# Inverse roots and key products moved from GpSimd to VectorE, and a written TensorE order of nineteen places rearranged, in a hybrid recurrent decoder step

## The chip, the cores and the metric

The kernel runs on one core of one Trainium2 chip. The metric is device time in microseconds for one launch. Three runs of the kernel before took 2502.68, 2503.41 and 2505.58 us. Engine names are those of the profile: PE is the matrix engine (TensorE), PEld its weight loads, DVE is VectorE, ACT is ScalarE, POOL is GpSimd, SP is SyncE, whose queue issues the transfers named here.

## The reference, cut to what matters

One layer of a decoder for 1024 prompt tokens and 8 x 4 sample tokens: a norm, a wide projection `w_in`, three token mixers side by side (gated DeltaNet, called A; RWKV-7, called B; a diagonal recurrence, called C), gates and output projection, then a feed-forward part. The change touches the two mixers that carry a matrix state:

```
def gated_delta_chunked(q, k, v, g, beta, S0):      # A: 4 heads of 128, after l2norm of q and k
    L = where(strict, einsum(kb, k) * decay, 0);  A = eye + L
    sol = triangular_solve(A, [v*beta, kb*exp(gc)], lower, unit_diagonal)
    ... scan over chunks: S = S*glast + kdec^T vnew ...
    o = o * rsqrt(mean(o*o) + EPS) * norm_g * silu(z)
def rwkv7_scan(r, w, k, v, kk, a, S0):               # B: 8 heads of 64, kk = l2norm(k * k_k)
    S = S*w + (S @ -kk) (kk*a)^T + v k^T;  o = S r
    o = (o - mean) * rsqrt(var + B_LN_EPS) * ln_w + ln_b ...
```

Three inverse square roots are in the chunked part: over the key norm of A, over the output norm of A, and over the group norm of B. The "beta products" of the change are the two scaled key matrices of B (`kk*a` and `k`, each times a growing exponential).

## The kernel before, in words

Matrix products in single precision are split in three (high times high, high times low, low times high), 128 x 352 columns each. The program has a start, the C mixer, then the chunked stretch of the A and B mixers, then the branch, output and feed-forward products. The change lies in the chunked stretch alone, from about 330 to 1480 us of the profile.

There the tokens are cut in segments, nine for each of two groups of heads (eight of 128 tokens and one of the 32 sample tokens), so 18 units of work. A unit consists of three Python generators: `rwkv_seg` (B, L1000), `gdn_seg` (A, L1282) and `tri` (the inverses of the triangular matrices of both, L906). Every `yield` ends a step. A fourth generator, the filler, hands out the big projection products that are not yet done, three 128 x 352 products at a time: first those that the second group of heads needs, then the gates.

A list `PLAN` (L1474) of 19 places says what the loop at L1478 emits in each place for the unit that is starting (`n`) and for the unit before it (`o`): `r`, `g` and `t` advance one generator by one step, and two filler steps (six products) follow in each place. The class `Ordered` (L249) pins the order of all matmuls: PE runs them exactly as written, so a matmul whose input is late holds all later ones. The other engines and the SP queue are ordered by a planner at build time; `o` steps and the inverse have high priority there. Each engine then runs its own queue in order.

The steps that matter, by their lines. B: r1 projections, decay and the products BK (L1078 to L1085); r2 the scores (BK against AR, L1091) and the masked matrix GM (L1095); r3 and r4 value terms; r5 to r10 the recurrence over two halves (state product, triangular product, state update; UV is written at L1185 and L1186, N at L1217 and L1218); the last part of r10 is the group norm with its root (L1227 to L1236); r11 transposes the normed output (L1242), gates it and stores it (L1245 to L1249). A: g1 transposes and the key root (L1318), g2 scores LA (L1339), g3 to g5 the state and the output root (L1423), g6 transposes and the gate (L1430). Inverse: `inv16_load` (L832) sends GM and LA through memory and reads 16 x 16 blocks (tile i16m), `inv16_solve` (L848) inverts the blocks on DVE (L858 to L886), stores them (L894) and reads them back (tile i16u, L897); t1 expands and transposes them (L923, L924) and makes the first product, t2 to t6 the rest. The step `unit` starts the loads of the next unit.

In the list before, numbered from 0, the scores r2 and `load` stand in place 7, r9 and g5 in place 6, r10 in place 8, `solve` in 11, g6 in 12, r11 in 14, t1 in 17 and t2 in 18; t3 to t6 stand in places 0 to 3 of the next round.

`rsqrt` (L641) starts from an integer estimate and makes three Newton steps, 13 instructions on two or four columns, all on POOL.

Of the kernel before, what the change touches and what calls it, by code (L numbers as in the profile page):

```python
# [10 lines left out]
I32 = mybir.dt.int32  # L11
AXX = mybir.AxisListType.X
AF = mybir.ActivationFunctionType
ALU = mybir.AluOpType
# [414 lines left out]
def build(tc, ap):  # L429
    nc = tc.nc  # L430
    with ExitStack() as ctx:
        k = K(tc, ctx, ap)
        V, A, P, T, S = k.V, k.A, k.P, k.T, k.S
# [195 lines left out]
        def big(n=NT):  # L629
            return k.tile(mp, [128, n], "a4", 6)  # L630
# [4 lines left out]
        def k1(shape=(128, SEG), tag="k1", bufs=6):  # L635
            return k.tile(mp, shape, tag, bufs)
# [4 lines left out]
        def rsqrt(x, shape, tag):  # L641

            yi = k.tile(mp, shape, "nwy" + tag, 2, I32)
            t = k.tile(mp, shape, "nwt" + tag, 1)
            P.tensor_scalar(out=yi, in0=x.bitcast(I32), scalar1=-0.5, scalar2=1597463007.0, op0=ALU.mult, op1=ALU.add)
            y = yi.bitcast(F32)
            for _ in range(3):
                P.tensor_tensor(out=t, in0=y, in1=y, op=ALU.mult)
                P.tensor_tensor(out=t, in0=t, in1=x, op=ALU.mult)
                P.tensor_scalar(out=t, in0=t, scalar1=-0.5, scalar2=1.5, op0=ALU.mult, op1=ALU.add)  # L650
                P.tensor_tensor(out=y, in0=t, in1=y, op=ALU.mult)
            return y

        def store_tail(dst, z, sv, hist):
# [27 lines left out]
        t = big()  # L682
# [10 lines left out]
        for b0, nb in ((0, 4), (4, 4), (8, 1)):  # L693
            n = 32 if b0 == 8 else 128
            ps = k.tile(k.pr, [128, 4, 128], "rr", 4)
            for j in range(nb):
# [12 lines left out]
                        in1=gla[:32, 8:9].to_broadcast([32, 8, 4]), op=ALU.mult)  # L709
# [290 lines left out]
        def rwkv_seg(R, seg, J):  # L1000

            s2, lora = R["s2"], R["lora"]
            if True:
# [9 lines left out]
                zr, zk, zv = k1(tag="zr", bufs=2), k1(tag="zk", bufs=2), k1(tag="zv", bufs=2)  # L1013
# [6 lines left out]
                kk, tt = k1(), k1()  # L1020
# [52 lines left out]
                og = k1(tag="og", bufs=2)  # L1073
# [3 lines left out]
                for i in range(2):  # L1077
                    A.activation(out=pr(av, i), in_=pr(av, i), func=AF.Identity, scale=k.p("bka", 2 * s2 + i), bias=k.d("oka", 2 * s2 + i))  # L1078
                V.tensor_tensor(out=ch(zk), in0=ch(zk), in1=ch(av), op=ALU.mult)
                for src, j, e in ((kk, 0, P), (zk, 1, V)):  # L1080
                    for h in range(2):
                        e.tensor_tensor(out=BK[H[h], 0:nb, j if h == 0 else 1 - j, 0:tl], in0=ch(src)[H[h]], in1=ch(ei)[H[h]], op=ALU.mult)
                V.tensor_tensor(out=ar(1), in0=ch(zr), in1=ch(eg), op=ALU.mult)
# [10 lines left out]
                for h in range(2):  # L1094
                    V.tensor_tensor(out=GM[:, h, 0:nb], in0=ph[h],  # L1095
                                    in1=k.c("gms" if samp else "gm").unsqueeze(1).to_broadcast([128, nb, 128]), op=ALU.mult)
# [53 lines left out]
                for b in range(nb // 2):  # L1150
# [43 lines left out]
                    if samp:  # L1194
                        yield
                        for i in range(2):
                            p2 = k.tile(pq, [128, 512], "sr", 1)
                            for q in range(2):
                                ux = k.tile(mp, [128, 2, 4, 64], "ux", 1)
                                for h in range(2):  # L1200
                                    P.tensor_tensor(out=ux[:, h], in0=UV[:, i, h].unsqueeze(1).to_broadcast([128, 4, 64]),
                                                    in1=k.c("uvm")[:, 4 * q:4 * q + 4].unsqueeze(2).to_broadcast([128, 4, 64]), op=ALU.mult)
# [30 lines left out]
                V.tensor_reduce(out=mv[:, 1], in_=sq, axis=AXX, op=ALU.add)  # L1233
                V.tensor_scalar(out=mv[:, 1], in0=mv[:, 1], scalar1=1.0 / 64, scalar2=GN_EPS, op0=ALU.mult, op1=ALU.add)
                rs = rsqrt(mv[:, 1], [128, nb], "r")
                V.tensor_tensor(out=O, in0=O, in1=rs.unsqueeze(2).to_broadcast([128, nb, 64]), op=ALU.mult)  # L1236
                yield
# [44 lines left out]
        def gdn_seg(R, seg, J):  # L1282
# [3 lines left out]
            if True:  # L1286
# [22 lines left out]
                for b in range(nb):  # L1309
# [6 lines left out]
                    A.copy(kv[:n, :, b], ps[:n].rearrange("p (j c) -> p j c", j=4)[:, 0:3:2])  # L1316
                V.tensor_scalar(out=ss, in0=ss, scalar1=0.25, scalar2=EPS, op0=ALU.mult, op1=ALU.add)
                rk = rsqrt(ss[:, 0], [n, nb], "g")  # L1318
                sl = k.tile(mp, [128, 3, 2], "gsl", 2)[:n]
                V.tensor_tensor(out=sl[:, 0], in0=rk, in1=rk, op=ALU.mult)  # L1320
# [100 lines left out]
                V.tensor_scalar(out=oss[:n, :nb], in0=oss[:n, :nb], scalar1=1.0 / 128, scalar2=None, op0=ALU.mult)  # L1421
                V.scalar_tensor_tensor(out=oss[:n, :nb], in0=ss[:, 1], scalar=128.0 * EPS, in1=oss[:n, :nb], op0=ALU.mult, op1=ALU.add)
                rs = rsqrt(oss[:n, :nb], [n, nb], "o")  # L1423
                for b in range(nb):
                    A.activation(out=oa[:n, b], in_=oa[:n, b], func=AF.Copy, scale=rs[:, b:b + 1])
# [38 lines left out]
        def unit(i):  # L1464
            J = {}
            u = dict(J=J, r=rwkv_seg(rb, SEGB[i % 9], J), g=gdn_seg(ra, SEGA[i % 9], J), t=tri(J))
            next(u["r"])
            next(u["g"])
            return u
# [1 line left out]

        PLAN = (("nr ot", 2), ("ng ot", 2), ("ot or", 2), ("ot or", 2), ("or og", 2), ("or og", 2), ("or og ng", 2), ("nr load", 2),  # L1474
                ("or unit", 2), ("nr", 2), ("nr", 2), ("solve", 2), ("og", 2), ("", 2), ("or", 2), ("", 2), ("", 2), ("nt", 2),
                ("nt", 2))
        new, old = unit(0), None
        for i in range(19):  # L1478
            after_ = None
            for what, f in PLAN:  # L1480
                for w_ in what.split():
# [132 lines left out]
        for g in range(NG):  # L1614
# [4 lines left out]
            for j in range(8):  # L1619
# [4 lines left out]
                                                  op=ALU.subtract)  # L1624
# [3 lines left out]
        for fb in range(8):  # L1628
# [29 lines left out]
            for g in range(NG):  # L1658
# [3 lines left out]
                for j0, nj in ((0, 3), (3, 3), (6, 2)):  # L1662
                    yo = k.tile(fa, [128, NT], "ahi", 5)[:, :nj * GW].rearrange("p (j t) -> p j t", j=nj)
                    for j in range(nj):
                        V.scalar_tensor_tensor(out=yo[:, j], in0=x2[j0 + j][:, gl(g)], scalar=k.p("gf", j0 + j), in1=rs,  # L1665
                                               op0=ALU.mult, op1=ALU.mult)
# [18 lines left out]
```

## Time and profile before

| of the profiled execution | value |
|---|---|
| device time of that execution | 2511.07 us |
| span, first to last instruction | 2509.3 us |
| median of the three timed runs | 2503.41 us |
| PE busy | 2183.4 us (87%) |
| DVE busy | 1178.8 us (47%), 2490 instructions |
| ACT busy | 816.8 us (33%) |
| POOL busy | 512.2 us (20%), 1213 instructions |

A busy share is the time in which an engine executed something. "PEclk" is the clock granted to PE as a share of full speed: 1.00 is the upper level (2.4 GHz), 0.50 the lower (1.2 GHz). In rows of the timeline the brackets at the end give how long the engine was idle before the row, and what ended the idle time; a row with x32 merges 32 instructions. The profiled execution is one of its kind, 0.3% above the median of the timed runs.

### The profile page before, as it was taken

How to read it: one execution, taken by the hardware profiler on the slowest of the kernel's cores; microseconds unless marked ns; L12 is line 12 of the kernel's file. 1: busy time of each engine (PE TensorE's matmuls, PEld its weight loads, DVE VectorE, ACT ScalarE, POOL GpSimd, SP SyncE). 2: the span in 40 equal slices, each digit the busy share in tenths (PEclk: the TensorE clock that was granted, in tenths of full speed). 3: DMA queues.
4: the chain of work that ended last, by engine and by line, in shares of the span. 5: the costliest groups of instructions: out<-in, count | busy, mean ns of one | idle time of the engine just before them, and what ended most of it. 6: DMA issues, size and time to landing. Idle time of an engine off the chain costs nothing. (4 is left out here: it accounts for less than half of the span.)

```text
span 2509.3 us, 42716 instructions
## 1 busy us (share of the span) xinstructions
PE 2183.4 (87%) x16939; PEld 2042.7 (81%) x16939; DVE 1178.8 (47%) x2490; ACT 816.8 (33%) x1915; POOL 512.2 (20%) x1213
## 2 busy tenths in 40 slices
PE   8999987776667677777777899999999999999997
PEld 7998986666556565666656799999999999999997
DVE  7453353555555544455445205747433433333336
ACT  5564342333333332243333222225221221221224
POOL 2013233333324223233343220013000000000003
PEclk9999996888887887888888899999999999999999
DMA  4114331222222222222221335433111111111114
GB/s 132 67 57 135 101 100 57 77 66 55 56 60 69 62 66 77 57 68 64 62 55 50 106 129 193 151 120 109 43 46 48 47 47 43 51 43 47 47 44 148
DMA packets 171713, 191.59 MB, mean 76 GB/s; under 512 B 60853, under 2 KB 114293, under 8 KB 171513
## 3 DMA queue, kind: packets, MB, share of 16 engines
q1 hardware_dynamic: 171512, 188.87, 24.6%
q8 instruction: 133, 2.18, 0.4%
q14 instruction: 68, 0.55, 0.1%
HBM read 140.68 MB, written 48.13 MB: 75 GB/s over the span
## 5 line engine op out<-in xcount | busy, mean ns | idle before, releaser
L259 PE MATMUL g<-hhi,whi 128*128 128x352 f32 x2664 | 904.5, 346 | 15.3 <-DVE z L419 14.0
L259 PE MATMUL g<-hhi,wlo 128*128 128x352 f32 x2568 | 848.5, 330 | 0.9 <-POOL wlo L343 0.9
L259 PE MATMUL g<-hlo,whi 128*128 128x352 f32 x2472 | 819.3, 331 | 4.6 <-DVE hlo L561 3.4
L259 PEld LDWEIGHTS g<-hhi,whi 128*128 128x128 f32 x2664 | 516.4, 195 | 34.6 <-DVE z L419 16.1
L259 PEld LDWEIGHTS g<-hhi,wlo 128*128 128x128 f32 x2568 | 501.1, 195 | 2.2 <-POOL wlo L343 1.4
L259 PEld LDWEIGHTS g<-hlo,whi 128*128 128x128 f32 x2472 | 485.4, 196 | 9.3 <-DVE hlo L561 4.5
L342 ACT CAST whi<-wraw 128x512 fp32r<-128x512 f32 x326 | 200.9, 619 | 558.2 <-PE g L259 545.8
L259 PE MATMUL g<-ahi,wlo 128*128 128x352 f32 x768 | 248.4, 323 | 0.0
L259 PE MATMUL g<-ahi,whi 128*128 128x352 f32 x768 | 248.3, 323 | 0.0
L259 PE MATMUL g<-alo,whi 128*128 128x352 f32 x768 | 248.1, 323 | 0.0
L1586 POOL TENSOR_TENSOR acc<-acc,sq 128x352 f32<-128x352 f32 x36 | 37.2, 1033 | 913.3 <-ACT sq L1585 912.7
L343 DVE TENSOR_TENSOR wlo<-wraw,whi 128x512 fp32r<-128x512 f32 x216 | 151.6, 703 | 146.8 <-ACT whi L342 142.8
L343 POOL TENSOR_TENSOR wlo<-wraw,whi 128x512 fp32r<-128x512 f32 x110 | 147.4, 1343 | 338.9 <-ACT whi L342 322.6
L1647 DVE TENSOR_TENSOR x<-g,x 128x352 f32<-128x352 f32 x192 | 100.4, 524 | 201.1 <-PE g L259 201.1
L259 PE MATMUL rr<-ix,GM 32*32 32x32 f32 x816 | 19.0, 224 | 171.0 <-DVE ix L924 171.0
L259 PEld LDWEIGHTS rr<-ix,GM 32*32 32x32 f32 x816 | 14.7, 134 | 178.2 <-DVE ix L924 129.3
L259 PEld LDWEIGHTS g<-ahi,wlo 128*128 128x128 f32 x768 | 144.8, 189 | 0.1
L259 PEld LDWEIGHTS g<-ahi,whi 128*128 128x128 f32 x768 | 144.6, 188 | 0.2
L259 PEld LDWEIGHTS g<-alo,whi 128*128 128x128 f32 x768 | 144.6, 188 | 0.1
L1636 DVE TENSOR_TENSOR rl<-rl,g 128x352 f32<-128x352 f32 x96 | 49.8, 519 | 133.5 <-ACT rl L1635 133.5
L1635 ACT ACTIVATE rl<-g 128x352 f32<-128x352 f32 x96 | 44.4, 463 | 138.5 <-PE g L259 138.5
L1638 DVE TENSOR_TENSOR alo<-rl,ahi 128x352 fp32r<-128x352 f32 x96 | 50.4, 525 | 47.5 <-ACT ahi L1637 47.5
(354 smaller groups left out, 2920.6 us busy)
## 6 DMA issues: line engine op xcount, KB each, us to landing
wraw<-win SPq DMA_DIRECT2D x126, 256.0 KB, 2.7
wraw<-wdn SPq DMA_DIRECT2D x80, 256.0 KB, 2.6
wraw<-wup SPq DMA_DIRECT2D x64, 256.0 KB, 2.6
scr_t<-z SPq DMA_DIRECT2D x24, 528.0 KB, 3.2
tgl<-scr_t SPq DMA_DIRECT2D x24, 528.0 KB, 4.1
scr_za<-z SPq DMA_DIRECT2D x16, 528.0 KB, 3.0
wraw<-wout SPq DMA_DIRECT2D x32, 256.0 KB, 2.6
scr_zb<-z SPq DMA_DIRECT2D x12, 528.0 KB, 2.7
```

Source lines behind the costliest of these rows:

```text
L259: return self._pin(self.eng.matmul(*a, **kw))
L342: self.A.copy(hi, r3)
L343: self.lo_eng.tensor_tensor(out=lo, in0=r3, in1=hi.bitcast(F32), op=ALU.subtract)
L1586: (V if last else P).tensor_tensor(out=acc[g], in0=acc[g], in1=sq, op=ALU.add)
L1635: A.activation(out=rl, in_=ps, func=AF.Relu)
L1636: V.tensor_tensor(out=rl, in0=rl, in1=ps, op=ALU.mult)
L1638: V.tensor_tensor(out=b[:, gl(g)], in0=rl, in1=a[:, gl(g)].bitcast(F32), op=ALU.subtract)
L1647: V.tensor_tensor(out=x2[c][:, gl(g)], in0=ps, in1=x2[c][:, gl(g)], op=ALU.add)
```

## The change

The root goes from POOL to DVE and from 13 to 10 instructions, the two products of `kk` in BK go from POOL to DVE beside those of `zk`, and the list of places is written anew. In the new list r5 to r8 and t2 to t6 stand one place later, r9 and g5 move from place 6 to place 7, behind the scores r2 and `load`; r3 moves from 9 to 10, r4 from 10 to 11 behind `solve`, `unit` from 8 to 9, g6 from 12 to 13, t1 from 17 to 18. r2 and `load` stay in 7, r10 in 8. `or` is named eight times where it was seven; counted by steps, r11 comes to stand in place 9, and the eighth `or`, in place 15, finds its generator at the end.

```diff
-            P.tensor_scalar(out=yi, in0=x.bitcast(I32), scalar1=-0.5, scalar2=1597463007.0, op0=ALU.mult, op1=ALU.add)
+            V.tensor_scalar(out=yi, in0=x.bitcast(I32), scalar1=-0.5, scalar2=1597463007.0, op0=ALU.mult, op1=ALU.add)
             y = yi.bitcast(F32)
             for _ in range(3):
-                P.tensor_tensor(out=t, in0=y, in1=y, op=ALU.mult)
-                P.tensor_tensor(out=t, in0=t, in1=x, op=ALU.mult)
-                P.tensor_scalar(out=t, in0=t, scalar1=-0.5, scalar2=1.5, op0=ALU.mult, op1=ALU.add)
-                P.tensor_tensor(out=y, in0=t, in1=y, op=ALU.mult)
+                V.tensor_tensor(out=t, in0=y, in1=y, op=ALU.mult)
+                V.scalar_tensor_tensor(out=t, in0=t, scalar=-0.5, in1=x, op0=ALU.mult, op1=ALU.mult)
+                V.scalar_tensor_tensor(out=y, in0=t, scalar=1.5, in1=y, op0=ALU.add, op1=ALU.mult)
...
-                for src, j, e in ((kk, 0, P), (zk, 1, V)):
+                for src, j, e in ((kk, 0, V), (zk, 1, V)):
...
-        PLAN = (("nr ot", 2), ("ng ot", 2), ("ot or", 2), ("ot or", 2), ("or og", 2), ("or og", 2), ("or og ng", 2), ("nr load", 2),
-                ("or unit", 2), ("nr", 2), ("nr", 2), ("solve", 2), ("og", 2), ("", 2), ("or", 2), ("", 2), ("", 2), ("nt", 2),
-                ("nt", 2))
+        PLAN = (("nr ot", 2), ("ng ot", 2), ("ot", 2), ("ot or", 2), ("ot or", 2), ("or og", 2), ("or og ng", 2), ("nr load or og", 2),
+                ("or", 2), ("or unit", 2), ("nr", 2), ("solve nr", 2), ("", 2), ("og", 2), ("", 2), ("or", 2), ("", 2), ("", 2), ("nt", 2))
```

## Rows read from the trace of the kernel before

**Rows 1.** Waits, whole execution: who waited for whom, total us, times, longest.
```profile
PE rr L259 <- DVE ix L924: 171.0, 18, 12.6
DVE k L1236 <- POOL nwyr L651: 55.9, 17, 3.7
```
**Rows 2.** Instructions of L924: duration in ns, first and last start in us.
```profile
L924 DVE STREAM_TRANSPOSE ix<-ixt x18: 311/378/379, 380.3 to 1388.8; 128x192 f32<-128x192 f32 x16, 128x128 f32<-128x128 f32 x2
```
**Rows 3.** Timeline of PE, one round: start us, duration us, instruction, idle before.
```profile
1115.91 0.65 PE L259 MATMUL rr<-ix,GM 32*32 32x32 f32 x32 [10.21 <-DVE ix L924]
...
1132.26 0.45 PE L259 MATMUL sr<-UV,BT 128*64 128x64 f32 x8 [2.17 <-DVE UV L1186]
...
1138.90 0.45 PE L259 MATMUL sr<-tm,inv 64*64 64x64 f32 x8
...
1140.28 1.03 PE L259 MATMUL rr<-kq 128*128 128x256 f32 x4
1142.20 1.16 PE L259 MATMUL rr<-AR,BK 64*128 64x128 f32 x16
...
1145.12 0.40 PE L259 MATMUL sr<-UV,GM 128*64 128x64 f32 x8
...
1152.45 1.07 PE L259 MATMUL rr<-UV,GM 64*64 64x64 f32 x16 [3.56 <-ACT UV L1118]
...
1159.26 0.68 PE L259 MATMUL rr<-con,k 64*64 64x64 f32 x16
1169.76 0.65 PE L259 MATMUL rr<-ix,GM 32*32 32x32 f32 x32 [6.76 <-DVE ix L924]
```
**Rows 4.** Windows of that round: us, busy time by engine, PEclk, DMA share, GB/s.
```profile
1115.90:1119.10 3.20, 3.19 (x78) 2.74 (x82) 0.36 (x1) 0.00 (x0) 0.00 (x0) 0.50 0.03 5
1132.30:1136.50 4.20, 4.20 (x32) 3.75 (x34) 3.44 (x9) 0.63 (x2) 1.27 (x2) 0.60 0.14 34
```
**Rows 5.** Timeline of DVE in that round.
```profile
1131.03 0.66 DVE L1320 TENSOR_TENSOR gsl<-nwyg 128x2 f32<-128x2 f32 x1 [1.20 <-POOL nwyg L651]
...
1149.08 0.29 DVE L1217 TENSOR_TENSOR N<-sr,N 128x128 f32<-128x128 f32 x1 [4.40 <-ACT k L1193]
...
1149.82 1.23 DVE L1230 TENSOR_SCALAR mv<-mv 128x4 f32<-128x4 f32 x1
...
1156.35 0.43 DVE L1236 TENSOR_TENSOR k<-k,nwyr 128x256 f32<-128x256 f32 x1 [3.69 <-POOL nwyr L651]
1157.44 0.48 DVE L1430 SCALAR_TENSOR_TENSOR zg<-rr,d_hang,zg 128x256 f32<-128x256 f32 x1 [0.66 <-PE rr L262]
1157.84 0.16 DVE L858 COPY i16z<-i16m 48x8 f32<-48x8 f32 x1
...
1158.31 0.17 DVE L871 TENSOR_TENSOR i16z<-i16z,i16t 48x8 f32<-48x8 f32 x1
1158.51 0.16 DVE L872 TENSOR_TENSOR i16t<-i16z 48x8 f32<-48x8 f32 x1
```
**Rows 6.** Timelines of POOL and of ACT in that round.
```profile
1149.64 1.37 POOL L343 TENSOR_TENSOR wlo<-wraw,whi 128x512 fp32r<-128x512 f32 x1 [1.96 <-ACT whi L342]
...
1156.12 0.20 POOL L651 TENSOR_TENSOR nwyr<-nwtr,nwyr 128x4 f32<-128x4 f32 x1
...
1147.72 0.70 ACT L1425 ACTIVATE oa<-oa,nwyo 128x128 f32<-128x128 f32 x2 [4.31 <-POOL nwyo L651]
```
**Rows 7.** Instructions of L1082 on DVE, and of L1230: duration ns min/median/max.
```profile
L1082 DVE TENSOR_TENSOR BK<-zk,k x36: 216/422/2040, 355.1 to 1352.0; 64x256 f32<-64x256 f32 x32, 64x64 f32<-64x64 f32 x4
L1230 DVE TENSOR_SCALAR mv<-mv x18: 156/165/1239, 441.2 to 1411.2; 128x4 f32<-128x4 f32 x16, 128x2 f32<-128x2 f32 x2
```
**Rows 8.** The SP queue in that round: start us, duration of the issue, transfer.
```profile
1150.45 0.32 SPq L846 DMA_DIRECT2D i16m<-scr_i  x1
...
1162.65 0.83 SPq L1249 DMA_DIRECT2D scr_y<-k  x2
1164.31 0.33 SPq L894 DMA_DIRECT2D scr_i<-i16z  x1
```

## The prediction

> **What bounds the kernel now.** I read the page first: PE is busy 87% of the span, and the slices in which it drops to six or seven tenths are those of the chunked stretch. The waits name the reason: the matmuls of t1 waited 171.0 us in 18 waits for the transpose of L924 [rows 1]. That transpose runs from 380.3 to 1388.8 us [rows 2], so the 17 rounds last 59.3 us on average. Then I took one plain round of the second half apart, 53.85 us from t1 at 1115.91 to t1 at 1169.76 [rows 3]; the reader is to see there that PE, in a fixed order, stops three times: 2.17 us at r7, 3.56 at r4 and 6.76 at the next t1 (10.21 at the one before). The clock falls too: 0.50 for the 3.2 us behind the t1 wait, 0.60 over the 4.2 us behind the r7 wait [rows 4].
>
> I split the round at the scores r2 (1142.20): stretch A, t1 to r2, 26.29 us, and stretch B, r2 to t1, 27.56 us. In B two things run side by side. PE's own work is 27.56 - 6.76 - 3.56 = 17.24 us. The inverse takes the whole 27.56: scores, GM, through memory, solve from 1157.84, its store at 1164.31, t1 5.45 us later [rows 3, 5, 8]. So t1 waits for a chain that begins at r2, and what stands before r2 on PE costs time, while what stands behind r2 is free until the 6.76 us and the r4 wait are used up.
>
> Why does the chain take so long? The load of its blocks is issued 8.25 us behind r2 [rows 8], but the solve starts 15.64 behind it. Just ahead of it in DVE's queue stand L1236, which waited 3.69 us for POOL's root, and L1430 [rows 5]; the root's input was late because N (L1217) waited 4.40 us for an ACT copy, and ACT itself had waited 4.31 us for the other root on POOL [rows 5, 6]. DVE's wait on that root comes to 55.9 us over the program [rows 1].
>
> **The change part by part.** *Moved work.* One filler place, r9 and g5 go from A to B. The three places between r11's end (1159.94) and the t1 wait's start (1163.00) make 1.02 us a place; r9 and g5 run from 1138.90 to 1140.28, 1.38 us [rows 3]. So A loses 2.40 us of PE work and B gains it. t1 moves one place in the list, not two.
>
> *Roots.* Three per unit, 13 POOL instructions each, become 10 on DVE. Dependent small DVE instructions follow each other at 0.20 us (L871 to L872), so a root takes 2.0 us instead of the 3.69 and 4.31 for which DVE and ACT were seen waiting [rows 5, 6]. DVE gets 30 x 0.17 = 5.1 us per round more. In B this lies in time in which DVE waited (4.40 + 3.69). In A DVE gets one root and the two beta products, 2.0 + 2 x 0.42 = 2.84 us [rows 7], and loses its wait of 1.20 for POOL at L1320, which stood ahead of UV and hence of r7 [rows 5].
>
> *r11 behind r10.* This adds a wait. The old list gives r5 to r11 seven `or`, the new list eight, and r11 is the seventh in both, now in place 9. On PE one filler place (1.02) separates it from r10; behind it queue all fillers, r3, r4, g6 and t1. From r10's end it needs: the ACT copy, 0.4 (my estimate for a copy whose engine is free); from N at 1149.08 to the start of L1236's wait at 1152.66 3.58, less 1.07 by which L1230 ran over its median of 0.165 [rows 5, 7], so 2.5; the root 2.0; L1236 0.43. With 0.8 for sharing DVE with A's root (half of ten times 0.16) that is 6.1, and PE waits 5.1. No row shows this wait. From below it is 6.1 - 0.8 - 0.4 - 1.02 = 3.9 (no sharing, and the copy beside other work); from above the 6.5 us of the solve (1157.84 to its store at 1164.31) come on top if they go first [rows 5, 8]: 5.1 + 6.5 = 11.6. I take 5.1, nearest to the row that has every piece, and add 0.6 for a POOL cast as in L1230's row, half of 1.23: 5.7.
>
> L1230 is a DVE instruction of 4 columns that took 1.23 us while POOL's L343 ran from 1149.64 to 1151.01 [rows 5, 6]. The Trainium skill, SBUF — State Buffer, section "Who interferes with whom", says that DVE and GpSimd share one port pair as an exclusive lock, and that a DVE instruction with two SBUF inputs, not only one in a two-port mode, is held by a GpSimd instruction that reads SBUF. By it nine of ten instructions of the new root can be held, where the old root never was; the trace agrees in L1320, two inputs, 0.66 us for two columns beside POOL's key product [rows 5]. If each root in B met one whole cast of 1.37, the round would be 0.8 longer than I take it and the time 17 x 0.8 = 14 us higher.
>
> *Stretch B new.* PE: 17.24 + 2.40 + 5.7 = 25.3, with r4's wait gone (ACT no longer stands behind a POOL root) and its lower clock passed on to r11's wait. Inverse: r10 ends 3.32 + 1.38 = 4.70 behind r2, its root and product are through at 4.70 + 6.7 = 11.4, the load of 8.25 has time to land; the solve starts 4.2 earlier, so t1 is ready at 27.56 - 4.2 = 23.4. PE is the later one, B is 25.3, and t1's wait is gone. r11's stores leave the queue ahead of the inverse's store, but that store follows the solve at once in this round, so I count nothing.
>
> *Stretch A new.* 26.29 - 2.40. With no t1 wait the half clock behind it goes: 3.2 x 0.5 = 1.6 at most, nothing at least if t1 still waits; I take 1.2. r7's wait with its clock is 2.17 + 4.2 x 0.4 = 3.85; it goes wholly or not at all; I take half, 1.9, since DVE is fuller by 2.84 - 1.20. For the fuller DVE I add 1.0 elsewhere in A (r8 behind N, r2 behind BK; 0 to 1.64). A is 26.29 - 2.40 - 1.2 - 1.9 + 1.0 = 21.8.
>
> *Sum.* 21.8 + 25.3 = 47.1 against 53.85: 6.7 less. Eight rounds of the second half at 6.7 make 54. The nine rounds of the first half carry convolution and sample work on DVE; the mean of 59.3 shows that rounds differ, and I take half, 3.4, so 31. In the last round no inverse covers r11's wait: 5 more. Saved: 54 + 31 - 5 = 80 us. The profiled execution took 2511.07 us and would take 2431; carried over to the median of the runs, 2503.4 - 80 = 2423.
>
> **The rivals.** *Everything works in all rounds.* r7's wait goes wholly (another 1.9) and nothing is added in A (1.0), and the first half gains like the second: a round is 44.2, and 17 x 9.6 - 5 = 158 go, 2345. For it speaks that the same waits on POOL recur 17 times [rows 1]; against it that DVE is the fuller engine in A.
>
> *Slower: the inverse gets stuck behind PE's new wait.* L1430 reads g6's PSUM result and stands directly ahead of the solve in DVE's queue [rows 5]; g6 is now behind r11, r3, r4 and four filler places. If the planner keeps that order, the solve cannot start before PE has come there: r11 done at 4.70 + 6.7 + 0.7 = 12.1 behind r2, then four places (4.1), r3 and r4 (2.0, my estimate from r4's 1.07), the lower clock (1.5) and L1430 itself (0.5): 20.2, then 6.5 and 5.45 to t1. B is 32.1, A 26.29 - 2.40 - 1.9 + 1.0 = 23.0, the round 55.1, 1.3 longer: 17 x 1.3 + 5 = 27, 2530. It decides from a solve start of 19 behind r2. For it speaks the row, against it that in place order the solve now stands two places ahead of g6.
>
> *Half: r11's wait nears its upper end.* With the solve ahead of the root, PE waits 11.6 instead of 5.7: B 31.2, the round 53.0, which the last round's 11 us undo: 2503. With half of that excess the round is 50.1, and 8 x 3.8 + 9 x 1.9 - 8 = 40 go: 2463. I put 2480 for it.
>
> *The list does not do what it says.* If r11 stood in place 15, no wait would be added: B is then the inverse's 23.4, the round 45.2, 17 x 8.6 = 147 saved, 2356. That r10 and r11 are 13.74 us apart before, in places 8 and 14, agrees with my count [rows 3].
>
> **How the numbers follow.** Forecast 2423, chance 0.55 (its own range 2390 to 2455). Everything works, 0.15; list as named, 0.03; half, 0.12, of which 0.02 fall within 0.2% and 0.02 above; slower, 0.11; some wait that I don't see cancels the gain, 0.04, half of it within 0.2%. Faster 0.55 + 0.15 + 0.03 + 0.08 + 0.01 = 0.82, same 0.04, slower 0.14. 0.2% is 5 us, about what a measurement of this kernel can tell from no change. The range leaves out the slower case and the end of the best: 2365 to 2498.
>
> **What would show it.** Right: POOL has no L645 to L651, DVE has 540 instructions there; r11's matmuls wait some 5 to 6 us for L1236 in each round; t1's wait on L924 falls from 171 us to under 50; r7's and r4's waits shrink. Wrong: t1's wait stays above 100 us together with r11's wait; the solve starts later than 15 us behind r2; or r11 waits over 10 us.

## The result: 130 us less, and the profile after

The kernel after takes 2374.47 us in the median of four runs (2372.05 to 2380.62) against 2504.29 us of the kernel before on the same chip (2502.68 to 2505.58): ratio 0.9486, 95% interval 0.9466 to 0.9505. The forecast was 2423 (2365 to 2498), 81 us less; measured are 130 less. The time lies in the stated range, but outside the forecast's own range (2390 to 2455) and nearer to the rival "everything works", priced at 2345, than to 2423. The profiled executions went from 2511.07 to 2373.66 us.

The page of the kernel after, busy time by engine (share of the span, instructions):

```profile
PE 2154.1 (91%) x16939; PEld 2020.1 (85%) x16939; DVE 1221.5 (51%) x3066; ACT 818.8 (35%) x1915; POOL 327.9 (14%) x475
```

POOL lost 184 us and 738 instructions, DVE gained only 43 us and 576. PE did the same products in 29 us less busy time; the PEclk column of the windows below rises from 0.82 and 0.85 to 0.86 and 0.89.

The waits of the kernel after (who waited for whom, total us, times, longest), which answer to [rows 1]:

```profile
PE rr L259 <- DVE k L1235: 101.5, 17, 10.3
PE rr L259 <- DVE ix L923: 24.9, 5, 9.9
```

(L1235 is L1236 of before, L923 is L924: lines behind L651 stand one lower.) The reader is to see an exchange: t1's 171.0 us became 24.9, and r11 has a new wait of 101.5, 6.0 us in each of 17. The two together fell by only 45 us. More lies in PE's waits for UV: those of the recurrence fell from 27.5 to 4.4 us,

```profile
PE sr L259 <- DVE UV L1186: 27.5, 16, 4.8
PE sr L259 <- DVE UV L1185: 4.4, 6, 1.2
```

(before, then after), and r4's waits (ACT UV L1118 and L1119, 19.8 us before) are gone. The rest lies in smaller waits and in the clock.

Where it went is seen from the windows of the two halves, from the first t1 to the tenth and from there to the eighteenth (us; busy time by engine; PEclk, DMA share, GB/s). The kernel before, whose first and last t1 are in [rows 2]:

```profile
380.30:933.70 553.40, 398.97 (x4192) 337.95 (x4192) 290.60 (x729) 186.36 (x550) 189.54 (x525) 0.82 0.23 64
933.70:1388.80 455.10, 336.78 (x3678) 284.46 (x3678) 219.30 (x586) 143.06 (x457) 149.42 (x416) 0.85 0.23 62
```

The kernel after, whose first and last transposes start at 377.6 and 1252.6:

```profile
377.60:853.30 475.70, 380.08 (x4164) 322.21 (x4165) 310.70 (x1016) 185.20 (x548) 89.66 (x155) 0.86 0.26 72
853.30:1252.60 399.30, 328.56 (x3679) 276.89 (x3678) 238.86 (x843) 143.04 (x455) 71.11 (x87) 0.89 0.26 72
```

The first nine rounds became 77.7 us shorter (8.6 each), the last eight 55.8 (7.0 each). With 2.7 us ahead of the first t1 and 1.2 behind the last, this is the whole difference of the spans, 137.4 us. Over both windows PE's busy time fell by 27 us and its idle time by 106.

Cut at r2, all 17 rounds show where in the round the gain lies. From PE's t1 to r2 (stretch A) they took 32.6 us in the mean of the first half and 30.8 of the second; they now take 24.6 and 23.7. From r2 to t1 (stretch B) 28.9 and 26.2 became 28.6 and 26.2. The gain is in A; in B the moved work fills what the waits gave up.

Now a plain round of the second half, from t1 to t1 (the second to the sixth round of this half are plain; B is 2.0 us shorter in their mean, and 3.5 longer in the mean of the three others). PE of the kernel after, answering to [rows 3]:

```profile
1024.07 0.45 PE L259 MATMUL rr<-ix,GM 32*32 32x32 f32 x32
...
1033.07 0.28 PE L259 MATMUL rr<-iz,ixt 32*32 32x32 f32 x3 [1.21 <-DVE iz L943]
...
1038.46 0.45 PE L259 MATMUL sr<-UV,BT 128*64 128x64 f32 x8
...
1042.57 0.71 PE L259 MATMUL sg<-gtm,TT 128*128 128x128 f32 x4 [0.77 <-ACT gqs L1372]
...
1045.04 1.16 PE L259 MATMUL rr<-AR,BK 64*128 64x128 f32 x16
...
1049.43 0.40 PE L259 MATMUL sr<-UV,GM 128*64 128x64 f32 x8
1055.61 0.73 PE L259 MATMUL rr<-con,k 64*64 64x64 f32 x16 [4.62 <-DVE k L1235]
...
1061.02 0.68 PE L259 MATMUL rr<-UV,GM 64*64 64x64 f32 x16
...
1068.75 0.45 PE L259 MATMUL rr<-ix,GM 32*32 32x32 f32 x32
```

Of the three stops of before none is left: r7 (1038.46), r4 (1061.02) and t1 carry no bracket. One large new stop stands at r11, two small ones in A: 1.21 us ahead of the products on iz, a step of the inverse, and 0.77 at A's state update. Stretch A is 1045.04 - 1024.07 = 20.97 us, B 1068.75 - 1045.04 = 23.71, the round 44.7 where it was 53.85. The clock still falls once, behind r11's wait (windows of A, of B and of the time behind r11's wait: us, busy time, PEclk, DMA share, GB/s):

```profile
1024.07:1045.04 20.97, 18.76 (x298) 15.85 (x297) 14.79 (x48) 10.16 (x37) 2.99 (x4) 1.00 0.29 87
1045.04:1068.75 23.71, 19.09 (x171) 16.97 (x170) 14.33 (x59) 7.16 (x21) 4.48 (x5) 0.93 0.32 84
1055.61:1057.80 2.19, 2.19 (x21) 2.08 (x22) 2.09 (x8) 0.81 (x2) 0.00 (x0) 0.61 0.00 0
```

The next 2.2 us are at 0.61 too; 4.4 us at 0.61 cost 1.7 us of a round, as much as behind r7's wait before [rows 4]. A is at 1.00 throughout. DVE of the same round, answering to [rows 5]:

```profile
1053.13 0.17 DVE L645 TENSOR_SCALAR nwyr<-mv 128x4 int32<-128x4 int32 x1
...
1054.20 0.17 DVE L857 COPY i16z<-i16m 48x8 f32<-48x8 f32 x1
...
1054.95 0.15 DVE L650 SCALAR_TENSOR_TENSOR nwyr<-nwtr,nwyr 128x4 f32<-128x4 f32 x1
...
1055.14 0.41 DVE L1235 TENSOR_TENSOR k<-k,nwyr 128x256 f32<-128x256 f32 x1
...
1060.10 0.68 DVE L885 TENSOR_REDUCE i16z<-i16p 48x64 f32<-48x512 f32 x1
...
1064.07 0.48 DVE L1429 SCALAR_TENSOR_TENSOR zg<-rr,d_hang,zg 128x256 f32<-128x256 f32 x1 [2.96 <-PE rr L262]
1067.92 0.38 DVE L923 STREAM_TRANSPOSE ix<-ixt 128x192 f32<-128x192 f32 x1
```

The root (L645 to the last L650) takes 2.0 us and none of these rows waits for POOL. The solve starts at L857, 9.2 us behind r2 instead of 15.6, in the middle of the root, and ends at 1060.78. L1429, the gate of g6, now stands behind the solve. The transpose for t1 ends at 1068.30; t1 starts 0.45 us later. In this round PE and the inverse arrive nearly together; over all 18 t1 starts 2.9 us in the mean (0.06 to 9.5) behind the end of its transpose.

SP's queue, answering to [rows 8]:

```profile
1051.62 0.33 SPq L845 DMA_DIRECT2D i16m<-scr_i  x1
...
1060.70 0.80 SPq L1248 DMA_DIRECT2D scr_y<-k  x2
1061.59 0.37 SPq L893 DMA_DIRECT2D scr_i<-i16z  x1
...
1064.48 1.28 SPq L896 DMA_DIRECT2D i16u<-scr_i  x2
```

The load of the blocks is out 6.6 us behind r2 (8.25 before). But r11's stores (L1248) hold the inverse's store for 0.8 us, and its read (L896) follows 2.9 us later: from the store to t1's data 6.7 us, where [rows 3, 8] had 5.45 to t1.

### The profile page after: what moved, and what is told of

It reads as the page before. It is cut to its first block, busy times and chain, and to the rows that moved or that the text cites. A ratio compares the mean times of both kernels' runs of the same rounds, so it can differ in the third digit from the quotient of the medians.

```text
span 2371.9 us, 42540 instructions
## 1 busy us (share of the span) xinstructions
PE 2154.1 (91%) x16939; PEld 2020.1 (85%) x16939; DVE 1221.5 (51%) x3066; ACT 818.8 (35%) x1915; POOL 327.9 (14%) x475
## 4 chain that ended last, share of the span: by engine, by line
PE 75%; DVE 14%; ACT 4%; issue 3%; DMA 2%; POOL 1%; SPq 0%; DVEq 0%; ACTq 0%; POOLq 0%
PE g L259 65%; PE rr L259 6%; PE sg L259 2%; PE sr L259 2%; DVE i16p L879 1%; DVE z L1273 1%; ACT WA L1045 1%; DVE BK L1081 1%; PE rr L262 1%; DMA i16m<-scr_i 1%; DVE hf L530 1%; ACT whi L342 1%; DVE k L1074 0%; ACT WA L1051 0%; DVE nwtg L648 0%
## 5 line engine op out<-in xcount | busy, mean ns | idle before, releaser
L259 PE MATMUL g<-hhi,whi 128*128 128x352 f32 x2664 | 894.7, 342 | 9.2 <-DVE z L419 8.7
L259 PEld LDWEIGHTS g<-hhi,whi 128*128 128x128 f32 x2664 | 510.5, 193 | 30.7 <-DVE z L419 9.9
L259 PEld LDWEIGHTS g<-hhi,wlo 128*128 128x128 f32 x2568 | 495.4, 193 | 3.1 <-POOL wlo L343 2.3
L259 PEld LDWEIGHTS g<-hlo,whi 128*128 128x128 f32 x2472 | 479.4, 194 | 7.0 <-DVE hlo L561 3.1
L342 ACT CAST whi<-wraw 128x512 fp32r<-128x512 f32 x326 | 201.4, 620 | 512.4 <-PE g L259 498.0
L259 PE MATMUL rr<-con,k 64*64 64x64 f32 x272 | 18.4, 307 | 101.5 <-DVE k L1235 101.5
L259 PEld LDWEIGHTS rr<-con,k 64*64 64x64 f32 x272 | 15.1, 208 | 106.9 <-DVE k L1235 106.7
```

What stands on the lines that cost most here:

```text
L259: return self._pin(self.eng.matmul(*a, **kw))
L342: self.A.copy(hi, r3)
```

## Experiments

Times are medians; each ratio is against the kernel before on the same chip, with its 95% interval.

**The list alone.** Roots and beta products as before, only the new list.

```diff
-        PLAN = (("nr ot", 2), ("ng ot", 2), ("ot or", 2), ...
+        PLAN = (("nr ot", 2), ("ng ot", 2), ("ot", 2), ("ot or", 2), ...
```

> The new list alone; roots and the beta products of kk stay on POOL. My theory (the time of a round is stretch A plus the later of PE's path and the inverse in stretch B): r11 still stands in place 9, and a root of 3.7 us on POOL instead of 2.0 makes its wait 8 to 10 us; PE's path in B is 17.2 + 2.4 + 9 = 28.6 against 27.6 before, A loses 2.4 moved and 1.2 of clock, so a round is 51 to 52 instead of 53.9 and the whole 2455 to 2485 us. Rival (the list is the gain, the engine of the root does not matter): under 2410 us, with r11 waits near 6 us.

Measured: 2453.21 us, 0.9794 (0.9775 to 0.9812), 2 us below the range that I had expected. Halves 513.1 and 436.7 us, 40 and 18 less than before. The waits:

```profile
PE rr L259 <- DVE k L1236: 124.0, 15, 9.8
PE rr L259 <- DVE ix L924: 20.5, 6, 7.2
```

With the root on POOL r11 waits 8.3 us instead of 6.0. The list takes most of t1's wait away by itself, and pays for it at r11. The solve starts early already (8.0 us behind r2 in this plain round), but DVE stands inside it, waiting for POOL's root:

```profile
1046.60 0.16 DVE L858 COPY i16z<-i16m 48x8 f32<-48x8 f32 x1
...
1052.65 0.42 DVE L1236 TENSOR_TENSOR k<-k,nwyr 128x256 f32<-128x256 f32 x1 [4.57 <-POOL nwyr L651]
```

**The roots alone.** The old list, roots and beta products on DVE.

```diff
-            P.tensor_scalar(out=yi, ...
+            V.tensor_scalar(out=yi, ...
...
-                for src, j, e in ((kk, 0, P), (zk, 1, V)):
+                for src, j, e in ((kk, 0, V), (zk, 1, V)):
```

> The roots and beta products on DVE, the old list. My theory: the solve starts some 4 us earlier because DVE no longer waits for POOL's root, r4's and r7's waits shrink, and t1 still waits 4 to 8 us per round: a round is about 5 shorter, 2400 to 2430 us. Rival (without the list the solve is held by something else, the memory round trip or the filler's work): t1's wait stays near 9.5 us, 2470 to 2505 us.

Measured: 2403.55 us, 0.9591 (0.9574 to 0.9607). Halves 498.0 and 418.6. The wait at t1:

```profile
PE rr L259 <- DVE ix L923: 152.7, 18, 13.3
```

t1's wait stays, 8.5 us each where I had expected 4 to 8, and still the larger part of the gain is here: 101 us alone, the list 51 alone, 130 together. The mean of the last eight rounds tells what each part does to the inverse (us behind r2):

| kernel | solve starts | solve ends |
|---|---|---|
| before | 11.7 | 19.5 |
| list alone | 8.8 | 19.3 |
| roots alone | 9.5 | 17.0 |
| both | 9.4 | 16.2 |

Either part alone starts the solve early. Only with the root on DVE does it end early, since DVE then has no wait for POOL inside or ahead of it; and the list fills PE's wait at t1 with work. The roots were moved and shortened at once, and no run parts the two: the old root's steps follow each other on POOL at 0.28 us (13 of them from 1152.75 to 1156.32), so by my estimate ten would have taken 2.8 us there, against 3.6 for thirteen and 2.0 for ten on DVE.

**The beta product back on POOL.**

```diff
-                for src, j, e in ((kk, 0, V), (zk, 1, V)):
+                for src, j, e in ((kk, 0, P), (zk, 1, V)):
```

> As the changed kernel, but the two products of kk in BK back on POOL. My theory: BK is ready before r2 asks for it either way, so the time is within 0.5% of the changed kernel, 2365 to 2385 us. Rival (two-input instructions on POOL hold DVE in the full stretch A): r7 waits again by 1 to 2 us in each round and the time is 2395 to 2410 us.

Measured: 2374.86 us, 0.9478 (0.9459 to 0.9498), as expected: no difference from the kernel after (0.9486). The beta products have no part in the gain that these runs can tell.

**r11 later.** If r11's wait is what bounds B, putting r11 further back must give it back. Three runs, with r11 (the seventh `or`) moved from place 9 to 15, 12 and 11; the second is shown:

```diff
-                ("or", 2), ("or unit", 2), ("nr", 2), ("solve nr", 2), ("", 2), ...
+                ("or", 2), ("unit", 2), ("nr", 2), ("solve nr", 2), ("or", 2), ...
```

> As the changed kernel, but r11 in place 15 (the or of place 9 taken out, so that the or of place 15 does it). My theory: the 6.0 us for which PE waited at r11 in 17 rounds go, and t1 waits 2 to 4 us for the inverse instead, since that is ready 21 to 23 us behind r2 and PE's own path in B is 19.6: about 3 us less per round and 5 at the end, 2305 to 2335 us. Rival (the early r11 is what keeps DVE and the SP queue free for the inverse): t1 waits as long as r11 did, 2365 to 2400 us.

> As the changed kernel, but r11 in place 12, between place 9 of the change and place 15 of the run before. My theory, amended by that run (there the read of the inverse stood behind r11's stores in SP's queue, 4.4 us behind the inverse's store instead of 1.6, and t1 waited for it): PE has 5 to 6 us of other work between r10 and r11, so r11 waits under 2 us, its stores are through before the inverse's, and t1 waits 1 to 4 us: 2335 to 2360 us. Rival (any wait that goes at r11 comes back whole at t1, since a round is bound by the inverse): 2365 to 2380 us.

> As the run with r11 in place 12, one place earlier, behind r4. My theory: r11 waits 1 to 3 us, t1 1 to 3 us, 2335 to 2360 us. Rival (a round is bound by the inverse): 2365 to 2380 us.

| r11 in place | time, us | ratio | r11's wait | t1's wait | sum |
|---|---|---|---|---|---|
| 9 (after) | 2374.47 | 0.9486 (0.9466 to 0.9505) | 101.5 | 24.9 | 126.4 |
| 11 | 2379.15 | 0.9494 (0.9473 to 0.9514) | 73.7 | 47.1 | 120.8 |
| 12 | 2367.71 | 0.9447 (0.9430 to 0.9463) | 57.8 | 57.0 | 114.8 |
| 15 | 2372.67 | 0.9472 (0.9456 to 0.9487) | 24.2 | 90.1 | 114.3 |

I had expected 2305 to 2335 for place 15 and 2335 to 2360 for places 12 and 11; all three were wrong, and the rival held each time: what r11 no longer waits, t1 waits. The sum of the two waits stays within some 12 us in all four kernels. Place 12 is a little faster than 9 (their intervals just part); 11 and 15 are not told apart from it.

By stretches, r11 in 15 did shorten B, by 1.5 us in the mean of the 17 rounds, but A became 1.8 us longer. The reason stands in the windows of A and B of its plain round:

```profile
1017.95:1040.37 22.42, 21.29 (x297) 17.89 (x297) 14.86 (x48) 10.24 (x36) 1.99 (x3) 0.87 0.19 53
1040.37:1065.08 24.71, 19.28 (x171) 17.38 (x170) 15.16 (x59) 7.38 (x22) 3.67 (x5) 0.93 0.33 86
```

PE needs 21.29 us for A's products where the kernel after needs 18.76: with the wait back at t1, the lower clock behind it is back too (0.87 over A instead of 1.00). My expectation had left this out.

SP's queue in this round shows one more loss:

```profile
1056.91 0.33 SPq L893 DMA_DIRECT2D scr_i<-i16z  x1
...
1059.49 0.52 SPq L1014 DMA_DIRECT2D zv<-scr_zb  x1
1060.31 0.83 SPq L1248 DMA_DIRECT2D scr_y<-k  x2
1061.22 1.28 SPq L896 DMA_DIRECT2D i16u<-scr_i  x2
```

The store of the inverse is out as far behind r2 as in the kernel after (16.5 us), though r11 is no longer ahead of it, and its read now stands in the queue behind r11's stores and leaves 4.3 us behind it; 1.6 is what it needs where nothing stands between. Over 18 rounds the distance is 2.99 us in the mean, 2.16 in the kernel after.

**Clearing SP's queue.** Two ways: r11's stores from POOL's queue, or the read from POOL's queue; each with r11 in 15 and in 12.

```diff
-                    S.dma_start(scr["y"][1, 2 * s2 + i][:, tk], pr(O, i))
+                    P.dma_start(scr["y"][1, 2 * s2 + i][:, tk], pr(O, i))
```

> The kernel with r11 in place 15, and r11's two stores issued from POOL's queue (behind POOL's own product) instead of SP's. In the run with r11 in 15 the read of the inverse from memory is issued 2.99 us behind the store of the inverse in the mean of 18 rounds, 1.6 where nothing stands between; t1's wait was 90.1 us. My theory (SP's order holds the read, and t1 waits for it): the read follows at 1.6 to 2.0 us, t1's wait falls by 17 x 1.0 to 1.4 to 65-75 us, the time goes from 2373 to 2345-2360. Rival (the read is late because of the other entries in SP's queue, or something else in the chain of the inverse is as late): read at 2.5 or more, time 2365-2380.

> The kernel with r11 in place 12, and r11's two stores issued from POOL's queue instead of SP's. In the run with r11 in 12 the read came 2.52 us behind the store in the mean, 1.6 at least, and t1's wait was 57.0 us, r11's 57.8. My theory: the read follows at 1.6 to 2.0, which is worth at most 17 x 0.9 = 15 us where t1 is the later one, and less where r11's wait then grows: 2352-2364, and the best version so far. Rival: 2365-2375, no change.

Measured: 2366.63 us, 0.9451 (0.9437 to 0.9465), with r11 in 15; 2359.36 us, 0.9414 (0.9395 to 0.9434), with r11 in 12. The time of the second is as my theory had it, but the mechanism is not: the distance from store to read is 2.79 and 2.41 us, not under 2.0, and my time for the first is missed. SP's queue with r11 in 15 shows what took the place:

```profile
1053.79 0.33 SPq L893 DMA_DIRECT2D scr_i<-i16z  x1
...
1056.36 0.52 SPq L1014 DMA_DIRECT2D zv<-scr_zb  x1
1056.98 1.27 SPq L896 DMA_DIRECT2D i16u<-scr_i  x2
```

The next entry ahead of the read, a load into the tile zv, could not leave until r11's sum had read the old zv (L1245, 1055.91 to 1056.33). With the stores gone the same step of r11 holds the queue through another entry.

```diff
-                S.dma_start(u[H[h]], dr[h].rearrange("b p c -> p b c"))
+                P.dma_start(u[H[h]], dr[h].rearrange("b p c -> p b c"))
```

> The kernel with r11 in place 12 (as in the run with r11 in 12, 2367.7 us), and the read of the inverse (L896, tile i16u) issued from POOL's queue instead of SP's, so that no other entry of SP's queue can stand between the inverse's store and its read. In that run the read came 2.52 us behind the store in the mean of 18 rounds, 1.6 where nothing stood between. My theory (SP's order holds the read): the gap falls to 1.6 to 2.0, t1's wait from 57 to 42-50 us, the time to 2350-2362. Rival (POOL is as late, by a cast of 1.3 us or by its own issue of some 0.6 us a read, and what is won at t1 is lost at r11): gap 2.3 or more or a larger r11 wait, time 2362-2375.

> The kernel with r11 in place 15 (2372.7 us with the read on SP), and the read of the inverse issued from POOL's queue. There the read came 2.99 us behind the store in the mean, and t1's wait was 90.1 us with r11's only 24.2, so that what the read gains should show at t1 nearly whole: 17 x (1.0 to 1.4) = 17 to 24 us. My theory: gap 1.6 to 2.0, t1's wait 65-75 us, time 2348-2358. Rival: gap 2.3 or more, time 2362-2375.

Measured: 2376.15 us, 0.9478 (0.9462 to 0.9494), in 12; 2378.28 us, 0.9494 (0.9479 to 0.9509), in 15. The rival held, with times 1 to 3 us above its range: the distance is 2.57 and 3.02 us, at least 2.1 in every round, and t1's wait grew to 65.8 and 95.4. POOL with r11 in 15 and the read there:

```profile
1064.09 0.74 POOL L1246 TENSOR_TENSOR k<-k,og 128x256 f32<-128x256 f32 x1 [10.85 <-DVE k L1245]
...
1065.04 0.68 POOL L896 DMA_DIRECT2D i16u<-scr_i  x1
```

The store had left at 1061.03. POOL stood 10.85 us waiting for r11's sum and took the read only then: the same block, in another queue.

**What the convolution has to do with the first half.** Three of four taps of mixer A's convolution are left out for the second pair of heads, once in the kernel before, once in the kernel after.

```diff
-                                for w_ in range(1, 4):
+                                for w_ in range(1, 4 if pair == 0 else 1):
```

> The kernel before without three of the four taps of mixer A's convolution for the second group of heads (left out: 18 DVE instructions of 1.25 us and 18 small ones, all in the first half of the chunked stretch). Question: why the first nine rounds gained 8.7 us each and not 3.4. Theory: in them convolution instructions stood in DVE's queue inside the solve and ahead of it, and the change moved them out of its way; so without them the kernel before gets shorter by 15 to 35 us in the first half, nothing in the second: 2470 to 2490 us. Rival (they were hidden behind PE's waits): under 8 us, 2496 to 2506 us.

> The changed kernel without the same three taps. Theory: PE's path decides there, and the taps lie beside it; under 10 us shorter, 2364 to 2378 us. Rival (they cost here what they cost before): 15 to 35 us shorter, 2340 to 2360 us.

Measured: 2485.01 us, 0.9915 (0.9888 to 0.9942), from before; 2366.47 us, 0.9442 (0.9422 to 0.9462), from after; two executions each, both times as expected. The halves, first of before without taps:

```profile
380.20:910.80 530.60, 390.72 (x4192) 331.12 (x4192) 265.64 (x693) 186.41 (x550) 182.32 (x525) 0.84 0.24 67
910.80:1364.00 453.20, 334.40 (x3678) 281.42 (x3678) 219.42 (x588) 143.17 (x457) 149.01 (x416) 0.85 0.23 63
```

and of after without taps:

```profile
375.50:842.70 467.20, 380.72 (x4164) 323.19 (x4165) 283.05 (x979) 185.06 (x548) 85.93 (x155) 0.86 0.26 73
842.70:1245.30 402.60, 333.87 (x3679) 281.96 (x3679) 238.04 (x844) 142.81 (x455) 70.89 (x87) 0.88 0.26 71
```

The taps cost the first half 22.8 us before (553.4 - 530.6) and 8.5 after (475.7 - 467.2). Without them the change is worth 63.4 us in nine rounds, 7.0 each, which is what it is worth in a round of the second half with all taps (6.3 in these two runs). In that half no tap was left out, and still it differs by 1.9 and 3.3 us from the executions with all taps: so much the halves of single executions are uncertain.

## Why the prediction was right, and what it had too small

*The step that was mis-sized: the first nine rounds.* I took 3.4 us a round, half of 6.7, because convolution and sample work fill DVE there. They gained 8.6, and 9 x (8.6 - 3.4) = 47 us of the 57 that the sum misses (137 of the profiled executions against 80) are this term. The two runs without taps show that the plain gain of 7.0 holds in the first half undiminished, and that the convolution adds some 1.6 (1.3 by the medians). In the kernel before three solves of the first half have four, six and one tap between their own instructions; in the kernel after one solve has one. The round at 740 us shows it, DVE of the kernel before:

```profile
737.34 1.46 DVE L1236 TENSOR_TENSOR k<-k,nwyr 128x256 f32<-128x256 f32 x1 [3.55 <-POOL nwyr L651]
...
739.77 0.44 DVE L880 TENSOR_TENSOR i16p<-i16m,i16z 32x64 f32<-32x64 f32 x2
740.14 1.27 DVE L1274 SCALAR_TENSOR_TENSOR z<-z,par,z 128x1024 f32<-128x1024 f32 x1
741.33 0.27 DVE L883 TENSOR_REDUCE i16t<-i16p 32x32 f32<-32x128 f32 x1
741.53 1.26 DVE L1274 SCALAR_TENSOR_TENSOR z<-z,par,z 128x1024 f32<-128x1024 f32 x1
```

Two steps of the solve stand behind a tap of 1.3 us each, on the chain that t1 waited for; L1236 with its wait for POOL's root takes 5.0 us of the same solve. That solve lasted 15.6 us, 12.7 with the taps left out, and 6.3 in the same round of the kernel after. Over the nine rounds the taps make the solve 0.95 us longer before (9.52 against 8.57 in the mean) and 0.36 after (6.98 against 6.62). But this is not where the 1.6 us come from: after, the taps delay the start of the solve by more (1.6 us against 0.9), and from r2 to the end of the transpose they cost 1.8 us a round before and 2.1 after. Before, t1 started 0.1 us behind the transpose in every round, so every delay of the inverse counted; after, PE came to t1 3.6 us behind it in the mean without taps and 2.8 with them, so that 0.8 of the 2.1 were hidden. That makes B's part of the 1.6, 0.5 us. The other 1.1 lie in A, 0.7 longer before and 0.4 shorter after; why stays open. That the rounds of the first half differ was read rightly; that this must cost the change was a guess, and of the wrong sign.

*A plain round* was forecast at 47.1 us and measures 44.7; the last eight gain 7.0 in the mean, forecast 6.7. That these two agree is in part luck: A gains 7.0 in the mean where I had 4.5, B nothing where I had 2.3; in the five plain rounds it is 6.0 and 2.0. In the round shown A was 21.8 by my terms and is 20.97: r7's wait went wholly, where I took half, and its clock with it (1.9), and A stayed at the upper clock (0.4 more than I took), while small stops (1.21, 0.77 and one of 0.21 us) cost 2.2, where I had 1.0 for the fuller DVE. B was 25.3 and is 23.71: PE's own work 19.1 (23.71 - 4.62) for 19.6, r11's wait 4.62 for 5.7.

*"Everything works in all rounds"* came nearer than the forecast, though I gave it 0.15: r7's wait went wholly in the round shown and the first half gained like the second, as it said; its round was 44.2.

*The wait at r11* has its size: 6.0 us in the mean for 5.7, and its lower clock came as said. In the round shown it is 4.62: from r10's end (1049.83) to the end of L1235 (1055.55) 5.7 us pass for the 6.1 of my pieces, and no cast adds anything. So the mean hits 5.7 for another reason than the 0.6 for a cast. The longest is 10.3, near the upper bound of 11.6. The root at a cadence of 0.20 us takes 2.0 us, as read from L871 to L872 [rows 5].

*The port.* My 0.6 us in each round for a POOL cast beside the root was too much. Of 540 root instructions 22 ran over 0.3 us, each beside a POOL instruction, together 14.3 us over their usual 0.16, and in plain rounds of the second half none of r11's root. One of them, DVE of the kernel after:

```profile
680.25 1.25 DVE L648 TENSOR_TENSOR nwto<-nwyo 128x2 f32<-128x2 f32 x1
```

and POOL:

```profile
680.22 1.26 POOL L343 TENSOR_TENSOR wlo<-wraw,whi 128x512 fp32r<-128x512 f32 x1 [10.79 <-ACT whi L342]
```

Two columns take as long as the cast beside them. 21 of the 22 have two inputs, which nine of ten root instructions have. By that the trace agrees with the Trainium skill, SBUF — State Buffer, section "Who interferes with whom": a DVE instruction with two SBUF inputs is held by a GpSimd instruction that reads SBUF. The 14 us that I had worked out by it for one root is about what all three roots lost together. That the old root never was held is wrong: in the kernel before 31 of its 702 instructions on POOL ran over 0.3 us, together 10.4 us over their usual 0.20, each beside a DVE instruction (L648 at 668.38 took 1.27 us, beside a tap of the convolution).

*The inverse.* The solve starts 9.2 us behind r2, forecast 11.4, since it doesn't wait for the root but interleaves with it; the data of t1 are there 23.3 us behind r2 (1068.30), forecast 23.4. The two agree by luck: I counted nothing for r11's stores, but 0.8 us ahead of the inverse's store and 1.3 behind it are given back in SP's queue.

*PE the later one by 2 us.* In this round it is 0.45, in the mean of all rounds 2.9, and 13 of 18 t1 came without a wait. The runs with r11 in 11, 12 and 15 show that these few us are no reserve to be had by moving r11: PE then waits at t1 and pays there with the clock. The rival "list does not do what it says" priced r11 in place 15 at 2356; with r11 really there it was 2373, its plain round 47.2 us from transpose to transpose (22.9 to r2 and 24.3 behind it) where the rival had 45.2 (21.8 and 23.4); part of the second term is the read in SP's queue.

*The slower rival* did not come: the planner put g6's gate (L1429) behind the solve. *Half* did not come either: one r11 waited over 10 us, none the 11.6. *The last round* cost nothing: r11 waits there too, 5.3 us, yet the stretch behind the last t1 became 1.2 us shorter, where I took 5 us more; PE's idle time there grew by only 1.2 us (24.1 to 25.3), since other waits went, and its busy time fell by 2.4 (1096.4 to 1094.0).

*Of the signs of being wrong* one was badly drawn: t1's and r11's waits together are 126.4 us, over the 100 that it names, but the forecast itself had 17 x 5.7 = 97 at r11 alone.

*What stays open.* PE and the inverse now come to t1 within some 3 us of each other, and no run shortened the inverse by itself: both ways to free its read ended at another entry of the same step. The version with r11 in 12 and its stores on POOL beats both kernels (0.9414, its interval wholly below that of the kernel after); why it does is shown only as a time, since the read came hardly earlier. Nor does any run tell the move of the root from its shortening.

## What to carry to other kernels

Take a small chain of dependent instructions off the engine where two other engines' queues stand waiting for it: here that alone, with three instructions fewer in the chain, was worth 101 of 130 us, though the engine that took it over has more work. Before halving a gain in rounds with more work, ask whether that work stands on the chain that the change shortens; then the gain can grow there. When two chains of nearly equal length meet, moving a wait from one to the other is worth little, the more so as the lower clock moves with the wait; and moving a read to another queue helps only if nothing there waits for the same step.

## What was not expected of the hardware

A read that depends on a store through memory leaves SP 1.6 to 1.7 us behind it at best (kernel after, 8 of 18), but POOL's queue 2.1 to 2.2 at best (the two runs with the read there), and each issue there takes 0.65 us of POOL's time.

One of the 22 held instructions has a single input, the first of a root, DVE of the kernel after:

```profile
621.54 0.66 DVE L645 TENSOR_SCALAR nwyg<-gss 128x2 int32<-128x2 int32 x1
```

It ends at 622.20, with POOL's cast that ran from 620.82 to 622.18; other L645 take 0.17. I had counted it among those that can't be held, though L1230, the row that I started from, has one input too: in the kernel before five of its 18 ran 0.83 to 1.24 us for a median of 0.165, each beside a POOL instruction.
